# A decoder layer on one core: squares of the first norm off GpSimd and later, set-up of the samples' retention later, first key cache in steps, and the third up-projection pair's weight sums later

## The chip, the cores and the metric

One core of one Trainium2 chip runs the whole program. TensorE (PE) multiplies, VectorE (DVE) and GpSimd (POOL) do elementwise work, ScalarE (ACT) does activations and casts, and SyncE (SP) issues the transfers. Each engine works through its own queue in order and waits on semaphores for the others. The metric is the device time of one execution in microseconds; lower is better.

## The reference

One layer of a decoder for a prompt of 1024 tokens and 8 samples of 4 tokens, D = 1024, with the same weights (`D_FF` = 2816):

```python
h = _rmsnorm(x, norm_g)
p = h @ w_in
q, k, v, g, su, sv, xq, gt = jnp.split(p, cuts, axis=-1)
o_ret, S_new = _retention_branch(q, k, v, g, pos, S0, ret_gn_g, ret_chunk)   # 4 heads, rotary, decay, GroupNorm, silu(g)
o_sg, v_rows = _sgu_branch(jax.nn.gelu(su), jax.nn.gelu(sv), sg_ln_g, sg_ws, sg_bs)
o_x = _xattn(q=xq, mk, mv)          # 4 heads into 256 memory tokens; the samples have caches of their own
merged = sig(g_ret) * (o_ret @ w_br_ret) + sig(g_sg) * (o_sg @ w_br_sg) + sig(g_x) * (o_x @ w_br_x)
x = x + merged @ w_o
z = _rmsnorm(x, norm_ffn_g) @ w_up
a, b = split(causal_conv3(z))
x = x + (gelu(a) * b) @ w_down
y = _rmsnorm(x, norm_final_g)
```

Outputs are y for prompt and samples, the retention and convolution states, the memory keys and values, and the samples' gating rows. All of it is float32.

## The kernel before

**Data.** Prompt and samples lie side by side as T = 1056 columns, feature-major: eight tiles of 128 x 1056 in SBUF hold x (`xr[0..7]`). A float32 product is made of three matmuls on a high and a low part of each operand (`hh`, `hl` of the activations, `wh`, `wl` of the weights). Weights come in slabs of 512 KB (`w_dma`), ACT casts the high part and POOL subtracts for the low part (`w_prep`; a `wl<-wr,wh` row of POOL is one such split). A unit is one k-tile of one product: nine matmuls, three of them over each piece of the columns.

**Order.** Python code writes each engine's queue in advance; nothing is reordered later. Main products go unit by unit (`fm2` for q and k of head 0 interleaved, `fm` for others, `tm` token-major for V), and after each unit `hook()` advances the generators in `gens` by `rate` steps, one generator after the other, and runs what `later(n, ...)` put off by n units. `drain()` runs all steps that are left. Product tiles in PSUM (`mp`) have two buffers in the first half of the program, small ones (`ap`) two, the FFN's (`bp`) three.

**Entry.** For each x tile ACT writes `hh` and DVE writes `hl`. Then the tiles are squared in place and summed to `xr[7]`; `rstd_all` casts the sum to `rsh` (ACT), subtracts for `rsl` (DVE), sums over features by matmuls with ones, and makes `rst` = 1/rms with a Newton step (`rms`, `ry`). The norm is applied behind the products, so q, k and g of head 0 can run on raw x; V and later products need `rtok`, which is `rst` transposed. The generator `xnorm` does the part from `xr[4]` on, a step at a time, starting after `YA` units, and `YB` steps lie between squares and sum.

**Retention.** `retention(h, ...)` runs as a generator beside the next products: A (scores of a chunk pair, masked into `rt`), B (`rt` times V, the state's part), C (the gated result `ort`), and SA, SB, SC, SD for the samples. SA makes the samples' scores and the masked copies `s` and `kdm` that SC multiplies. The order of these steps is a tuple in the code.

**Gating unit and cross-attention.** `sgu` mixes channel groups: PE makes `ap<-sgW,vg`, DVE adds (`sgt`) and multiplies (`su`). `KS(h, i)` splits half of a head's cached keys (`kch` cast by ACT, `kcl` by POOL); `xattn` is a generator of 20-odd steps a head, in which `YA(i)` uses them.

**FFN.** The up-projection goes in pairs of 512 columns with seven products instead of eight: a11, a12, s4, s2, s3, s1, a22, where the s are sums of weight blocks (`f_sums`) and each part is split by `f_prep0` (a11, a12), `f_prep1` (s2, s3), `f_prep2` (s1, s4) and `f_prep3` (a22). `put` and `z_put` add a product in PSUM to tiles `zt`, `zu`, `z` on DVE. In pair 1, the second, DVE also still makes parts of the normed activations (`xl<-x2c,xh`); `Conv` steps follow the convolution of the pair before. The list `early1` says what of pair 1's weights is prepared in which unit of the last products ahead of the FFN.

Of the kernel before, what the change touches and what calls it, by code (L numbers as in the profile page):

```python
# [10 lines left out]
AF = mybir.ActivationFunctionType  # L11
ALU = mybir.AluOpType
# [66 lines left out]
def step_kernel(ctx: ExitStack, tc: tile.TileContext, xT, memT, wslab, cst, ident_d, rope, vec, sgc, sgm, sgs,  # L79
# [10 lines left out]
    def slot(name, dt=F32, shape=None):  # L90
        return sp.tile(shape or [P, T], dt, tag="S", name=name, bufs=NSLOT)
# [16 lines left out]
    def act(out, in_, func=AF.Identity, scale=1.0, bias=0.0, **kw):  # L108
        nc.scalar.activation(out=out, in_=in_, func=func, scale=scale, bias=bias, **kw)  # L109

    def vtt(out, a, b, op):
        nc.vector.tensor_tensor(out=out, in0=a, in1=b, op=op)  # L112

    def ptt(out, a, b, op):
        nc.gpsimd.tensor_tensor(out=out, in0=a, in1=b, op=op)  # L115
# [4 lines left out]
    def f(t):  # L120
        return t.bitcast(F32) if t.dtype == F32R else t
# [50 lines left out]
    gens = deque()  # L172
# [112 lines left out]
    def split(src, name, sub=ptt):  # L285
        shape = list(src.shape)
        hi = slot(name + "h", F32R, shape)
        lo = slot(name + "l", F32R, shape)
        nc.scalar.copy(out=hi, in_=src)
        sub(lo, src, f(hi), ALU.subtract)  # L290
        return hi, lo
# [60 lines left out]
    with tc.manual_schedule():  # L352
# [9 lines left out]
        xr = [slot("xr") for _ in range(8)]  # L362
# [43 lines left out]
            x_part(k, slice(0, T))  # L406

        for k in range(4):
            ptt(xr[k], xr[k], xr[k], ALU.mult)
            for a, b in {1: ((1, 0),), 3: ((3, 2), (3, 1))}.get(k, ()):  # L410
                ptt(xr[a], xr[a], xr[b], ALU.add)
        for i in range(2):
            hil[SLABS[i]] = first[i]
        wst.update(d=2, p=2, live=2)
# [8 lines left out]
        nc.vector.tensor_scalar(out=vecs[:, VBG:VBG + 32], in0=vecs[:, VBG:VBG + 32], scalar1=0.5, scalar2=None,  # L423
                                op0=ALU.mult)

        YA, YB = 5, 6

        def xnorm():
            for _ in range(YA):
# [64 lines left out]
        def retention(h, qt, kt, silu, V, st, s3, s0, s0s):  # L494
# [156 lines left out]
                    stt(ot[e][:, TP:T], a[:, e * 32:e * 32 + 32],  # L651
                        vecs[:, VGN + 2 * h + e:VGN + 2 * h + e + 1], silu[e][:, TP:T], ALU.mult, ALU.mult)

            for fn, *a in ((int,), (A, 0), (SA,), (A, 1), (B, 0), (B, 1), (SC, 0), (B, 2), (C, 0), (SC, 1), (A, 2), (B, 3),
                           (SB, 0), (B, 4), (C, 1), (A, 3), (B, 5), (SD,), (B, 6), (C, 2), (SB, 1), (B, 7),
                           (SB, 2), (SB, 3), (C, 3)):
                while defer:
                    defer.pop(0)()
                fn(*a)
                yield  # L660
# [217 lines left out]
        def sgu():  # L878
            for _ in range(3):
                yield  # L880
            for half in range(2):
                for g in range(4):
                    a = ap()
                    for n in range(4):
                        mm(a[:, n * P:(n + 1) * P], vt(4 * half + n)[:, g * P:(g + 1) * P], sgW[:, g * P:(g + 1) * P])
                    t = slot("sgt")
                    vtt(t[:, 0:512].rearrange("p (a b) -> p a b", a=4), a.rearrange("p (a b) -> p a b", a=4),
                        sgC[:, g * P:(g + 1) * P].unsqueeze(1).to_broadcast([P, 4, P]), ALU.add)
                    s = su[g][:, half * 512:(half + 1) * 512]
                    vtt(s, s, t[:, 0:512], ALU.mult)  # L890
                    yield
                if half == 0:
                    vc_load(0)
            a = ap()
            for g in range(4):
                mm(a[:, g * 32:g * 32 + 32], sgS[0:32, 512 + g * P:512 + (g + 1) * P],
                   sgS[0:32, 256 + 32 * g:256 + 32 * g + 32])
            t = slot("sgt")
            vtt(t[:, 0:128], a[:, 0:128], sgC[:, 512:640], ALU.add)
            for g in range(4):  # L900
                ptt(su[g][:, TP:T], su[g][:, TP:T], t[:, g * 32:g * 32 + 32], ALU.mult)
                later(4, lambda g=g: dma(scr[8 + g], su[g]))
            yield
# [25 lines left out]
        def KS(h, i):  # L929
            if h < H:  # L930
                ksl.setdefault(h, {})[i] = split(kcl[h][i], "kc")
# [184 lines left out]
        later(4, lambda: dma(sgv, sgS[0:32, 512:1024]))  # L1116
        rate[0] = 1.05
        gens.append(sgu())
        KS(0, 0)
        KS(0, 1)  # L1120
        gens.append(xattn(0))
        for m in range(1, 4):
            xq_unit(m)
# [76 lines left out]
        for m in range(8):  # L1200
# [4 lines left out]
            for half in range(2):  # L1205
                t = slot("mg", F32R)
                src = acc[m][:, half * HW:(half + 1) * HW]
# [73 lines left out]
        fraw, fw = {}, {}  # L1281
# [4 lines left out]
                for t, key in zip(fraw[j], (("up", j), ("up", NFF + j))):  # L1286
                    dma(t, wslab[SLABS.index(key)])

        def f_parts(j, names, src, own=False):
            if own:  # L1290
                hi, lo = slot("fh", F32R, [P, 1024]), slot("fl", F32R, [P, 1024])
            else:
                hi = wp.tile([P, 1024], F32R, tag="wh", name="wh", bufs=3)
                lo = wp.tile([P, 1024], F32R, tag="wl", name="wl", bufs=3)
            nc.scalar.copy(out=hi, in_=src)  # L1295
            ptt(lo, src, f(hi), ALU.subtract)
            for i, n in enumerate(names):
                fw[j][n] = (hi[:, 512 * i:512 * i + 512], lo[:, 512 * i:512 * i + 512])

# [5 lines left out]
        def f_sums(j, sub, sub34=ptt):  # L1305

            a11, a12, a21, a22 = f_quads(j)
            fsum[j] = (slot("fs"), slot("fs"))
            s2, s3, s1, s4 = [t[:, 512 * i:512 * i + 512] for t in fsum[j] for i in range(2)]
            sub(s1, a21, a22, ALU.add)  # L1310
            sub(s2, s1, a11, ALU.subtract)
            return lambda: (sub34(s3, a11, a21, ALU.subtract), sub34(s4, a12, s2, ALU.subtract))

        def f_prep0(j, own=False):
            fw[j] = {}
            f_parts(j, ("a11", "a12"), fraw[j][0], own)

        def f_prep1(j, own=False):
            f_parts(j, ("s2", "s3"), fsum[j][0][:, 0:1024], own)
# [4 lines left out]
        def f_prep3(j):  # L1324
            a22 = f_quads(j)[3]
            t = slot("f22", F32R)
            nc.scalar.copy(out=t[:, 0:512], in_=a22)
            ptt(t[:, 512:1024], a22, f(t)[:, 0:512], ALU.subtract)
            fw[j]["a22"] = (t[:, 0:512], t[:, 512:1024])
            del fraw[j]  # L1330
            if j > 1:
                f_dma(j + 1)


        def raw1():
            fraw[1] = [slot("fr", shape=[P, 1024]) for _ in range(2)]
            for t, key in zip(fraw[1], (("up", 1), ("up", NFF + 1))):
                dma(t, wslab[SLABS.index(key)])

        early1 = [int, lambda: f_prep0(1, True), lambda: f_sums(1, vtt, vtt)(), int, lambda: f_prep3(1),  # L1340
                  lambda: f_prep1(1, True), int, int]

        for half in range(2):
            rate[0] = 0.25
            for m in range(8):
                key = ("wo", m, half)
                hi, lo = w_get(key)
# [38 lines left out]
        def prod(w, name, ps=None, start=True, stop=True, tick=None):  # L1386


            if ps is None:
                ps = bpp.tile([P, 2, 512], F32, tag="bp", name="bp", bufs=3)  # L1390
            ch = ((0, 0, HA), (1, HA, HB)) if name in ("B12", "B22", "T1") else ((0, 0, QW), (1, QW, QW))
            wh, wl = [x.rearrange("p (k c) -> p k c", c=P) for x in w]
            for k in range(4):
                xh, xl = xop(name, k)
                for i, (a, r) in enumerate(((wh, xh), (wh, xl), (wl, xh))):
                    for q, c0, n in ch:
                        mm(ps[:, q, 0:n], a[:, k, :], r[:, c0:c0 + n], start=(start and k == 0 and i == 0),
                           stop=(stop and k == 3 and i == 2))
                if tick:
                    tick()  # L1400
            return ps

        def put(ps, out, tmp=None):
            if tmp is None:
                nc.scalar.copy(out=quarters(out), in_=ps[:, :, 0:QW])
            else:
                vtt(quarters(out), ps[:, :, 0:QW], quarters(tmp), ALU.add)
# [9 lines left out]
        def z_put(ps, half, z, zs, tmp=None):  # L1417

            if half == 0:
                put(ps, z[:, 2:2 + HW], tmp)  # L1420
                return
            oz = n496(z[:, 2 + HW:2 + TP])
            if tmp is None:
                nc.scalar.copy(out=oz, in_=ps[:, :, 0:HA])
                nc.scalar.copy(out=zs[:, :, 2:6], in_=by4(ps[:, 1, HA:HB]))
            else:
                vtt(oz, ps[:, :, 0:HA], n496(tmp), ALU.add)
                vtt(zs[:, :, 2:6], by4(ps[:, 1, HA:HB]), by4(tmp[:, 2 * HA:HW]), ALU.add)
# [51 lines left out]
        A = lambda k: (h_scale(k, 1), x_split(B1(k), k % 4, h(k, 1), None))  # L1480
# [84 lines left out]
        d = fw.pop(1)  # L1565
        p1, r, u3, u4 = blocks(1)
        put(prod(d["a11"], "B11", tick=do), p1)
        f_prep0(2)
        n = prod(d["a12"], "B21", tick=do)
        za = z_new(1)  # L1570
        z_put(n, 0, *za, p1)
        n = prod(d["s4"], "B22", tick=do)
        z_put(n, 1, *za)
        f_sums(2, ptt)()
        put(prod(d["s2"], "T2", tick=do), r, p1)
        f_prep1(2)
        pa.first()
        pa.tap(1)
        put(prod(d["s3"], "T3", tick=do), u3, r)
        pa.tap(0)  # L1580
        pa.gelu()
        f_prep2(2)
# [34 lines left out]
        for j in range(2, NFF):  # L1617
# [4 lines left out]
            d = fw[j]  # L1622
# [4 lines left out]
            p1, r, u3, u4 = blocks(j)  # L1627
# [355 lines left out]
```

## Time and profile before

| | |
|---|---|
| time, median of 3 runs | 1944.57 us (1942.96 to 1952.96) |
| profiled execution, its own time | 1949.1 us |
| span in the trace, mean granted clock | 1947.3 us, 0.987 |
| busy PE, DVE, POOL, ACT | 1878.4, 1078.1, 927.7, 615.9 us |
| HBM read, written | 137.04, 35.43 MB |

The span is from the first to the last instruction of the profiled execution; the 1.8 us between it and that execution's time lie outside. Rows of the timeline give start, duration in us, engine, line, operation, output<-inputs, shape, how many were joined (x6 means six in a row), and in brackets the engine's idle time before it and what ended that.

### The profile page before, as it was taken

Reading aid. Unit: us, or ns where it says so; the run is one execution under the profiler, and the core shown is the slowest. Engines: PE = TensorE matmul, PEld = TensorE weight load, DVE = VectorE, ACT = ScalarE, POOL = GpSimd, SP = SyncE. Lnnn points to the kernel's source line nnn. Section 1 sums busy time; section 2 is a strip of 40 time slices with the busy share of each in tenths; the row PEclk is TensorE's granted clock in tenths of the full one; section 3 lists DMA queues with packets and bytes.
Section 4 is the critical chain, followed back from the end, with each engine's and each line's share of the span. In section 5 each row is a group of like instructions: output and inputs, shape, how many; then the busy total and the mean of one; then the engine's idle time right before and its main releaser. Section 6 shows DMA issues by size and latency. Waiting matters only on the chain.

```text
span 1947.3 us, 31390 instructions
## 1 busy us (share of the span) xinstructions
PE 1878.4 (96%) x13201; PEld 1852.8 (95%) x13201; DVE 1078.1 (55%) x1506; ACT 615.9 (32%) x962; POOL 927.7 (48%) x576
## 2 busy tenths in 40 slices
PE   7999999999989999999999999899999999999997
PEld 6999999999989999999999999899999999999996
DVE  8463636443375541111112247999999999744446
ACT  5232232322234332111132233534434334321204
POOL 6242424232544334333154434477777777753404
PEclk9999999999999999999999999899999999999998
DMA  5112121324142313111221443022222222742202
GB/s 184 55 44 91 44 91 44 132 68 153 55 133 77 109 45 133 55 44 54 89 84 48 164 153 99 33 66 89 77 66 89 77 84 95 264 142 89 75 1 90
DMA packets 51741, 174.51 MB, mean 90 GB/s; under 512 B 5712, under 2 KB 8944, under 8 KB 51600
## 3 DMA queue, kind: packets, MB, share of 16 engines
q1 hardware_dynamic: 51600, 172.50, 26.3%
q8 instruction: 104, 1.70, 0.4%
q14 instruction: 37, 0.30, 0.1%
HBM read 137.04 MB, written 35.43 MB: 89 GB/s over the span
## 4 chain that ended last, share of the span: by engine, by line
PE 80%; DVE 11%; ACT 3%; issue 3%; DMA 1%; POOL 1%; SPq 0%; DVEq 0%; ACTq 0%; POOLq 0%
PE mp L106 55%; PE bp L106 20%; PE ap L106 4%; DVE xl L112 1%; DVE c L118 1%; DVE x2c L118 1%; DVE hl L118 1%; DVE s L112 1%; DMA xr<-in_xT 1%; DMA scr<-ox 0%; ACT sw L476 0%; DVE rt L118 0%; DVE st L526 0%; SPq L103 0%; PE ap L576 0%
## 5 line engine op out<-in xcount | busy, mean ns | idle before, releaser
L115 POOL TENSOR_TENSOR wl<-wr,wh 128x1024 fp32r<-128x1024 f32 x114 | 296.7, 2605 | 463.6 <-ACT wh L150 391.2
L106 PE MATMUL mp<-hh,wh 128*128 128x384 f32 (+1 forms) x1152 | 264.2, 337 | 9.7 <-DVE q L112 4.9
L106 PE MATMUL mp<-hl,wh 128*128 128x384 f32 (+1 forms) x1152 | 254.1, 328 | 4.8 <-DVE hl L118 4.8
L106 PE MATMUL mp<-hh,wl 128*128 128x384 f32 (+1 forms) x1152 | 251.8, 326 | 0.0
L106 PE MATMUL bp<-xh,wh 128*128 128x264 f32 (+2 forms) x1040 | 211.4, 284 | 1.0 <-DVE x2c L118 0.9
L106 PE MATMUL bp<-xl,wh 128*128 128x264 f32 (+2 forms) x1040 | 211.1, 284 | 0.0
L106 PE MATMUL bp<-xh,wl 128*128 128x264 f32 (+2 forms) x1040 | 211.0, 284 | 0.0
L106 PEld LDWEIGHTS mp<-hh,wh 128*128 128x128 f32 x1152 | 192.9, 192 | 12.9 <-ACT hh L109 5.3
L106 PEld LDWEIGHTS mp<-hl,wh 128*128 128x128 f32 x1152 | 193.5, 190 | 7.2 <-DVE hl L118 7.2
L106 PEld LDWEIGHTS mp<-hh,wl 128*128 128x128 f32 x1152 | 193.8, 190 | 0.0
L112 DVE TENSOR_TENSOR x<-x,mp 128x288 f32<-128x288 f32 (+3 forms) x167 | 105.7, 675 | 121.3 <-PE mp L106 121.3
L106 PEld LDWEIGHTS bp<-xh,wh 128*128 128x128 f32 x1040 | 162.4, 188 | 1.4 <-issue 1.4
L106 PEld LDWEIGHTS bp<-xl,wh 128*128 128x128 f32 x1040 | 162.4, 188 | 0.0
L106 PEld LDWEIGHTS bp<-xh,wl 128*128 128x128 f32 x1040 | 162.3, 188 | 0.0
L115 POOL TENSOR_TENSOR wl<-fs,wh 128x1024 fp32r<-128x1024 f32 x41 | 119.0, 2902 | 55.7 <-ACT wh L1295 55.7
L150 ACT CAST wh<-wr 128x1024 fp32r<-128x1024 f32 x100 | 103.9, 1041 | 78.7 <-PE mp L106 50.0
L106 PE MATMUL mp<-ach,whs 128*128 128x384 f32 (+3 forms) x524 | 124.3, 326 | 3.9 <-DVE x L112 3.1
L118 DVE SCALAR_TENSOR_TENSOR c<-z,hist,c 128x1024 f32<-128x1024 f32 x88 | 124.6, 1416 | 4.2 <-ACT c L109 2.5
L112 DVE TENSOR_TENSOR th<-mp,rst 128x768 f32<-128x768 f32 (+1 forms) x48 | 31.6, 701 | 170.9 <-PE mp L106 150.3
L106 PE MATMUL mp<-acl,whs 128*128 128x384 f32 (+3 forms) x524 | 124.1, 327 | 0.0
L106 PE MATMUL mp<-ach,wls 128*128 128x384 f32 (+3 forms) x524 | 124.0, 326 | 0.0
L118 DVE SCALAR_TENSOR_TENSOR th<-th,mp 128x768 f32<-128x768 f32 (+1 forms) x48 | 31.7, 701 | 145.4 <-PE mp L106 145.4
(356 smaller groups left out, 4107.9 us busy)
## 6 DMA issues: line engine op xcount, KB each, us to landing
wr<-in_wslab SPq DMA_DIRECT2D x162, 512.0 KB, 3.6
sca<-c SPq DMA_DIRECT2D x22, 528.0 KB, 3.0
opr<-sca SPq DMA_DIRECT2D x22, 528.0 KB, 4.5
opr<-scr SPq DMA_DIRECT2D x16, 528.0 KB, 5.4
scr<-ort SPq DMA_DIRECT2D x8, 528.0 KB, 7.6
x2c<-in_xT SPq DMA_DIRECT2D x8, 528.0 KB, 7.7
scx<-x2c SPq DMA_DIRECT2D x16, 264.0 KB, 3.5
x<-scx SPq DMA_DIRECT2D x8, 528.0 KB, 6.9
```

What stands on the lines that cost most here:

```text
L106: nc.tensor.matmul(out=out, lhsT=l, rhs=r, start=start, stop=stop)
L112: nc.vector.tensor_tensor(out=out, in0=a, in1=b, op=op)
L115: nc.gpsimd.tensor_tensor(out=out, in0=a, in1=b, op=op)
L118: nc.vector.scalar_tensor_tensor(out=out, in0=a, scalar=s, in1=b, op0=op0, op1=op1)
L150: nc.scalar.copy(out=hi, in_=raw)
```

## The change

Six edits.

```diff
         for k in range(4):
-            ptt(xr[k], xr[k], xr[k], ALU.mult)
+            act(xr[k], xr[k], AF.Square)
             for a, b in {1: ((1, 0),), 3: ((3, 2), (3, 1))}.get(k, ()):
-                ptt(xr[a], xr[a], xr[b], ALU.add)
+                vtt(xr[a], xr[a], xr[b], ALU.add)
...
-        YA, YB = 5, 6
+        YA, YB = 14, 3
...
-            for fn, *a in ((int,), (A, 0), (SA,), (A, 1), (B, 0), (B, 1), (SC, 0), (B, 2), (C, 0), (SC, 1), (A, 2), (B, 3),
+            for fn, *a in ((int,), (A, 0), (A, 1), (B, 0), (SA,), (B, 1), (SC, 0), (B, 2), (C, 0), (SC, 1), (A, 2), (B, 3),
...
         gens.append(sgu())
-        KS(0, 0)
-        KS(0, 1)
+
+        def first_keys():
+            for i in range(2):
+                KS(0, i)
+                yield
+                yield
+
+        gens.append(first_keys())
         gens.append(xattn(0))
...
-        early1 = [int, lambda: f_prep0(1, True), lambda: f_sums(1, vtt, vtt)(), int, lambda: f_prep3(1),
+        s34q = []
+        f_s12 = lambda: s34q.append(f_sums(1, vtt, vtt))
+        early1 = [int, lambda: (f_prep0(1, True), f_s12()), lambda: s34q[0](), int, lambda: f_prep3(1),
                   lambda: f_prep1(1, True), int, int]
...
         put(prod(d["a11"], "B11", tick=do), p1)
-        f_prep0(2)
         n = prod(d["a12"], "B21", tick=do)
         za = z_new(1)
         z_put(n, 0, *za, p1)
+        f_prep0(2)
         n = prod(d["s4"], "B22", tick=do)
         z_put(n, 1, *za)
+        put(prod(d["s2"], "T2", tick=do), r, p1)
         f_sums(2, ptt)()
-        put(prod(d["s2"], "T2", tick=do), r, p1)
-        f_prep1(2)
         pa.first()
         pa.tap(1)
         put(prod(d["s3"], "T3", tick=do), u3, r)
+        f_prep1(2)
```

`f_parts` and `f_prep0` also get a parameter `sub` for the subtracting engine, with the engine of before as default, which no call sets. Four squares go from POOL to ACT and three adds from POOL to DVE. The rest of the norm starts nine units later and has three steps fewer before its sum. SA stands behind B(0). The first two key splits become steps behind the gating unit's steps. Pair 1's first two sums stand a unit earlier than the other two. In pair 1, the preparation of pair 2 is issued later.

What stands in the queues there. First DVE at the entry, from just behind the six `hl` (`xr<-xr` are the adds of the sum of squares, `q` and `k` the evacuations of their products, `sw` the rotated half):

```order
+L112 TENSOR_TENSOR xr<-xr 128x1056 x3
 L423 TENSOR_SCALAR vecs<-vecs 128x32
-L112 TENSOR_TENSOR xr<-xr 128x1056 x4
 L112 TENSOR_TENSOR q<-mp,cosT 128x768
 L112 TENSOR_TENSOR q<-mp,cosT 128x288
-L112 TENSOR_TENSOR rsl<-xr,rsh 128x1056
+L112 TENSOR_TENSOR xr<-xr 128x1056
 L112 TENSOR_TENSOR k<-mp,cosT 128x768
 L112 TENSOR_TENSOR k<-mp,cosT 128x288
 L112 TENSOR_TENSOR q<-q,sw 128x1056
-L309 TENSOR_SCALAR rms<-ap 128x384
+L112 TENSOR_TENSOR xr<-xr 128x1056 x3
```

Three adds stand ahead of q's evacuation, one behind it and three behind k's; `rsl` follows them.

POOL at the end of the gating unit (`sgS` is the samples' part, `su` the samples' last multiplies), before:

```order
L115 TENSOR_TENSOR sgS<-sgS,sgW 32x512
L115 TENSOR_TENSOR kcl<-kc,kch 128x1024 x2
L115 TENSOR_TENSOR wl<-wr,wh 128x1024 x3
L115 TENSOR_TENSOR su<-su,sgt 128x32 x4
L115 TENSOR_TENSOR wl<-wr,wh 128x1024
L115 TENSOR_TENSOR vcl<-vc,vch 128x1024 x2
```

and now:

```order
L115 TENSOR_TENSOR sgS<-sgS,sgW 32x512
L115 TENSOR_TENSOR wl<-wr,wh 128x1024 x3
L115 TENSOR_TENSOR su<-su,sgt 128x32 x4
L115 TENSOR_TENSOR kcl<-kc,kch 128x1024 x2
L115 TENSOR_TENSOR wl<-wr,wh 128x1024
L115 TENSOR_TENSOR vcl<-vc,vch 128x1024 x2
```

The two key splits moved behind three weight splits and the samples' multiplies.

POOL in pair 1 (`z` and `zs` are the convolution's input tiles, `fs` the sums, `wl<-wr` here f_prep0's split, `wl<-fs` those of f_prep1 and f_prep2), before:

```order
L115 TENSOR_TENSOR wl<-wr,wh 128x1024
L1433 MEMSET z 128x2
L1434 COPY zs<-hist 128x8x2
L115 TENSOR_TENSOR fs<-wr 128x512
L115 TENSOR_TENSOR fs<-fs,wr 128x512
L115 TENSOR_TENSOR fs<-wr 128x512
L115 TENSOR_TENSOR fs<-wr,fs 128x512
L115 TENSOR_TENSOR wl<-fs,wh 128x1024 x2
```

and now:

```order
L1441 MEMSET z 128x2
L1442 COPY zs<-hist 128x8x2
L115 TENSOR_TENSOR wl<-wr,wh 128x1024
L115 TENSOR_TENSOR fs<-wr 128x512
L115 TENSOR_TENSOR fs<-fs,wr 128x512
L115 TENSOR_TENSOR fs<-wr 128x512
L115 TENSOR_TENSOR fs<-wr,fs 128x512
L115 TENSOR_TENSOR wl<-fs,wh 128x1024 x2
```

On POOL only f_prep0's split changed its place, by two small operations; the sums wait for other DVE operations than before, since the slots that they write come free in another order. On ACT the cast of f_prep1 (`wh<-fs`) stood ahead of the convolution's first activations (`c`):

```order
L1233 CAST xh<-x2c 128x528 x4
L1295 CAST wh<-fs 128x1024
L109 ACTIVATE c<-z,hist 128x1024
L109 ACTIVATE c<-zs,hist 128x32
L1455 COPY coll<-z 128x2
L1456 COPY coll<-zs 128x16
```

and stands behind them now:

```order
L1239 CAST xh<-x2c 128x528 x4
L109 ACTIVATE c<-z,hist 128x1024
L109 ACTIVATE c<-zs,hist 128x32
L1463 COPY coll<-z 128x2
L1464 COPY coll<-zs 128x16
L1301 CAST wh<-fs 128x1024
```

It moved behind four operations of ACT.

More of the change, by code (lines that the diff above doesn't have):

```diff
@@ L1287, in f_dma, with f_parts @@
                     dma(t, wslab[SLABS.index(key)])
-        def f_parts(j, names, src, own=False):
+        def f_parts(j, names, src, own=False, sub=ptt):
             if own:
@@ L1295, in f_parts @@
             nc.scalar.copy(out=hi, in_=src)
-            ptt(lo, src, f(hi), ALU.subtract)
+            sub(lo, src, f(hi), ALU.subtract)
             for i, n in enumerate(names):
@@ L1312, in f_sums, with f_prep0 @@
             return lambda: (sub34(s3, a11, a21, ALU.subtract), sub34(s4, a12, s2, ALU.subtract))
-        def f_prep0(j, own=False):
+        def f_prep0(j, own=False, sub=ptt):
             fw[j] = {}
-            f_parts(j, ("a11", "a12"), fraw[j][0], own)
+            f_parts(j, ("a11", "a12"), fraw[j][0], own, sub)
         def f_prep1(j, own=False):
```

## The prediction

> **What bounds the kernel.** I read the busy shares, then the chain of waits of TensorE, then each long wait in the timelines of the engines beside it.
>
> ```profile
> PE 1878.4 (96%) x13201; PEld 1852.8 (95%) x13201; DVE 1078.1 (55%) x1506; ACT 615.9 (32%) x962; POOL 927.7 (48%) x576
> PEclk9999999999999999999999999899999999999998
> ...
> PE ap L106 <- DVE sgt L112: 7.6, 1, 7.6
> PE bp L106 <- DVE zt L112: 6.9, 1, 6.9
> PE ap L106 <- DVE rt L118: 5.4, 3, 2.6
> PE mp L106 <- DVE q L112: 4.9, 1, 4.9
> ...
> PE mp L106 <- DVE hl L118: 4.8, 7, 1.7
> ...
> PE mp L106 <- DVE x2c L118: 2.8, 1, 2.8
> ```
>
> TensorE (PE) is busy 1878.4 of 1947.3 us, so 69 us of idle time is all that a reordering can reach, plus matmuls that run at a lower granted clock after an idle stretch. No matmul is added or removed. The second block is who ends PE's waits (total, times, longest): VectorE (DVE) nearly always. The change lies at the first five; they sum to 29.6 us. So the question at each is why DVE is late there, and what is late next.
>
> **Entry: squares off GpSimd (POOL), rest of the norm later.**
>
> ```profile
> 10.78 1.32 DVE L118 SCALAR_TENSOR_TENSOR hl<-xr,vecs,hh 128x1056 fp32r<-128x1056 f32 x1 [0.46 <-ACT hh L109]
> ...
> 13.23 18.96 DVE L118 SCALAR_TENSOR_TENSOR hl<-xr,vecs,hh 128x1056 fp32r<-128x1056 f32 x6
> ...
> 32.20 9.18 DVE L112 TENSOR_TENSOR xr<-xr 128x1056 f32<-128x1056 f32 x4
> ...
> 42.54 2.19 DVE L112 TENSOR_TENSOR rsl<-xr,rsh 128x1056 fp32r<-128x1056 f32 x1
> ...
> 12.18 18.90 POOL L115 TENSOR_TENSOR xr<-xr 128x1056 f32<-128x1056 f32 x6 [2.81 <-DVE hl L118]
> ...
> 36.74 0.65 PE L106 MATMUL mp<-hl,wh 128*128 128x384 f32 x3
> 37.23 0.65 PE L106 MATMUL mp<-hh,wl 128*128 128x384 f32 x3
> 42.76 1.22 PE L106 MATMUL mp<-hh,wh 128*128 128x384 f32 x3 [4.89 <-DVE q L112]
> ...
> 70.58 0.28 PE L106 MATMUL mp<-wh,hh 128*128 128x256 f32 x1
> ...
> 43.00:48.00 5.00, 5.00 (x18) 5.00 (x19) 4.99 (x4) 4.02 (x6) 3.83 (x3) 0.50 0.34 105
> ```
>
> One hl takes 1.32 us alone and 3.16 (18.96/6) while POOL's six squares and adds run; the two trade places, each held up by the other. Then four xr adds (9.18 us) stand ahead of q's evacuation, and PE, done with head 0's q and k at 37.88 (37.23 + 0.65), starts g only at 42.76. The granted clock in the next 5 us is 0.50: 2.5 us lost.
>
> After: POOL has no square here, so six hl at about 1.3 end near 13.2 + 7.9 = 21.1. The squares go to ScalarE (ACT), which already squares the other four tiles:
>
> ```profile
> 18.61 1.18 ACT L109 ACTIVATE hh<-xr,vecs 128x1056 fp32r<-128x1056 f32 x1
> 22.43 1.09 ACT L109 ACTIVATE xr<-xr 128x1056 f32<-128x1056 f32 x1 [2.64 <-DVE hl L118]
> ...
> 42.51 2.19 ACT L476 COPY sw<-mp 64x768 f32<-64x768 f32 x4
> 44.73 1.05 ACT L150 CAST wh<-wr 128x1024 fp32r<-128x1024 f32 x1
> ```
>
> Four more are 4.4 us behind ACT's last hh (18.61 + 1.18 = 19.8), so they end near 24.3, with the 2.64 of waiting gone; three adds behind them near 26, beside matmuls and well before q is to be evacuated. PE's hl waits (4.8) go: q and k end at 37.88 − 4.8 = 33.1, and g starts there, not at 42.76. From g's start to the first matmul of V PE took 70.58 − 42.76 = 27.8, 25.3 without the slow clock. With no new wait V would start at 58.4.
>
> New waits. The rstd matmuls stand in PE's queue behind the first unit of the second g half: nine units behind 33.1. Three matmuls start 0.49 after the three before them (36.74, 37.23), a unit is nine, so 1.46, and PE is there at 46.2. The sum they need is now made later: k's copies by ACT (2.2 behind 33.1), a weight cast and two squares (1.05 and 2 x 1.09) to 38.6, three adds, rsh (1.07), rsl. At 1.25 an add and 1.25 for rsl it is ready at 44.6. At 3.3 an add and 2.2 for rsl, with POOL's two wl and sw around, it is ready at 51.8. I take 48.5, near the middle: PE waits 2.3 (0 to 5.6). The clock falls behind such a wait:
>
> ```profile
> 205.69 1.62 PE L106 MATMUL ap<-V,rt 128*128 128x256 f32 x6 [2.64 <-DVE rt L118]
> ...
> 205.60:208.00 2.40, 2.31 (x9) 2.16 (x10) 1.22 (x4) 0.37 (x1) 0.55 (x2) 0.50 0.03 7
> ...
> 1182.85 0.72 PE L106 MATMUL mp<-mg,wh 128*128 128x264 f32 x4 [2.85 <-DVE x2c L118]
> ...
> 1182.00:1186.00 4.00, 3.15 (x26) 3.18 (x27) 3.29 (x5) 2.36 (x4) 1.59 (x1) 1.00 0.17 68
> ```
>
> A wait of 2.64 was followed by 0.50 for 2.4 us, one of 2.85 by none; I take 1.5. Last, the transposes for rtok now stand right before V, and V's first PSUM tile is the one g's first half gives back after rtok and two silu multiplies (2 x 0.65): 1.9 more. V starts at 58.4 + 2.3 + 1.5 + 1.9 = 64.1, **gain 6.5**; without the rsl wait 10.3, with 5.6 and 2.5 of clock 2.2.
>
> The Trainium skill, "TensorE: Matmul & The Clock Gate", section "What's actually happening", says that the clock halves after at least one idle window of about 3.4 us. The row at 205.69 differs (2.64, and 0.50 granted), the one at 1182.85 agrees; by the rule alone the 1.5 would go and the total be 18.
>
> **Samples' set-up (SA) later, four heads.**
>
> ```profile
> 106.75 2.46 DVE L112 TENSOR_TENSOR s<-s,cB 128x256 fp32r<-128x256 f32 x2
> ```
>
> SA's four DVE operations (1.54, 0.19, 2.46; the first and third beside POOL) stood ahead of the rt of A(1) that B(1) needs. Behind B(0) they delay SC(0) instead, one unit after B(1). The three rt waits (5.4) and some clock go. What comes instead: SA's first step on ACT starts one unit later, SC(0) stands two further on, so by my walk through each head's timeline 1.9, 0.8 and 2.0 of its chain stick out. I take **0**, between the full 5.4 + 1.5 with nothing new and −3, where all of the late chain sticks out.
>
> **First key cache in steps.**
>
> ```profile
> 538.03 10.57 DVE L112 TENSOR_TENSOR su<-su,sgt 128x512 f32<-128x512 f32 x1
> ...
> 549.23 0.69 DVE L112 TENSOR_TENSOR su<-su,sgt 128x512 f32<-128x512 f32 x1
> ...
> 538.79 4.66 POOL L115 TENSOR_TENSOR kcl<-kc,kch 128x1024 fp32r<-128x1024 f32 x2
> 543.42 4.62 POOL L115 TENSOR_TENSOR wl<-wr,wh 128x1024 fp32r<-128x1024 f32 x2
> ...
> 549.25 1.01 PE L106 MATMUL ap<-sgW,vg 128*128 128x128 f32 x3 [7.58 <-DVE sgt L112]
> ...
> 549.00:555.00 6.00, 5.75 (x29) 5.75 (x30) 3.87 (x7) 1.05 (x1) 0.70 (x1) 0.63 0.87 247
> ```
>
> One su multiply, 0.69 alone, takes 10.57: it is held until POOL's four splits, back to back, are over (543.42 + 4.62 = 548.04). PE resumes 1.2 us later and loses 2.2 to the clock. The change moves both kcl behind the gating unit's last step; two wl remain. If DVE is again held to the end of POOL's run, that is 538.8 + 4.6 = 543.4, PE resumes at 544.6: 4.6 gained and about 0.5 of clock, **5.1**. If it gets in behind the first, 2.3 more and all of the clock: 9.6. If the two casts, now issued without kch ahead, let the third wl in too, 2.4 less: 2.7.
>
> The kcl find POOL behind the four small su, near 562 to 567; the first matmul on them is four to five units behind the last step, where POOL has only wl. Cross-attention's steps come four units (5.8 us) later, and fit: 92 steps on 92.4 that the hooks of the remaining gate units give. Its last results are needed only after the first gc and all bs products. I take 0 (±2).
>
> The Trainium skill, "SBUF — State Buffer", section "Who interferes with whom", says that a VectorE instruction with two SBUF inputs and a GpSimd one that reads SBUF exclude each other for a whole instruction. The 10.57 agrees, but it outlasts four instructions, which the rule does not say; if one instruction were all, the total would be 21.
>
> **Pair 1's sums in two units.** PE's 2.85 at 1182.85 stays: DVE is full there, and the two early sums only change the order ahead of it. Two 0.7 us sums: **0** (±1.5).
>
> **Third pair's sums later.**
>
> ```profile
> 1235.27 14.57 DVE L112 TENSOR_TENSOR xl<-x2c,xh 128x528 fp32r<-128x528 f32 x10
> 1249.77 0.69 DVE L112 TENSOR_TENSOR zt<-bp,zt 128x528 f32<-128x528 f32 x1
> ...
> 1238.88 1.69 POOL L115 TENSOR_TENSOR fs<-wr 128x512 f32<-128x512 f32 x1 [1.26 <-DVE xl L112]
> ...
> 1246.79 2.48 POOL L115 TENSOR_TENSOR wl<-fs,wh 128x1024 fp32r<-128x1024 f32 x1 [1.10 <-ACT wh L1295]
> ...
> 1250.61 0.78 PE L106 MATMUL bp<-xh,f 128*128 128x264 f32 x2 [6.93 <-DVE zt L112]
> ...
> 1251.00:1257.00 6.00, 6.00 (x31) 6.00 (x31) 4.83 (x11) 3.65 (x5) 1.08 (x1) 0.54 0.01 3
> ```
>
> Ten xl, 0.70 alone elsewhere,
>
> ```profile
> 1172.15 0.70 DVE L112 TENSOR_TENSOR xl<-x2c,xh 128x528 fp32r<-128x528 f32 x1
> ```
>
> take 14.57, 7.6 too many, beside POOL's four sums (1238.88 to 1245.69) and its wl (1246.79 to 1249.27). The put of s2's product stands behind them and lets PE go at 1250.61, 6.93 late, and then at 0.54 of the clock for 6 us (2.8). After: the sums wait for a slot freed four DVE operations later, and the cast ahead of wl stands behind the convolution's first step, so wl (2.1 of the excess) and part of the sums leave. Some excess stays: f_prep0's wl is issued later and now meets the first xl. Put at about 1246.1 − 0.7: gain 4.4, and 0.5 of the clock, **4.9**. Bounds: 1, if wl and sums only change places, and 6.9 + 2.8 = 9.7. What is late next: nothing that I see; s3, s1 and a22 of the second pair stand between this place and the third pair's first product.
>
> **Sum.** 6.5 + 0 + 5.1 + 0 + 4.9 = 16.5. The profiled execution took 1949.1 us, so 1932.6 in such an execution; it lies 4.5 over the median of the runs, 1944.57, and against this I say **1928.1**.
>
> **Rivals.**
> Small gain: the entry's gain turns into the rsl wait (2.2), and su is held through a third wl (2.7), with 2 at the third pair: 6.8, time 1938. For it: each of my gains is at a place where the two engines share, and moving work has it meet the next operation.
> Large gain: DVE gets in between POOL's instructions, as hl did with POOL's squares at 13 to 32: 10.3 + 9.6 + 6 = 26 less 2 for SA, time 1921. Against it: su waited through four in a row.
> Slower: the norm's chain decides. All of V waits for rtok, which needs rsl, then the rstd matmuls, three Newton operations and the transposes. If POOL holds DVE there as it held su (10.57 for one operation) in two of the five operations after k's evacuation, rsl is ready near 48.5 + 20, PE waits 22 and loses 2.5 of clock: V starts at 58.4 + 22 + 2.5 + 1.9 = 84.8, 14.2 later than before, and with the 10.0 from the other places the time is 1949. It is slower than before once rsl is ready after about 64. Against it: POOL has only three instructions in that stretch (wl, sw, wl), not back to back.
> No effect: the third pair's wait is set by ACT's casts, not by POOL, and su by its PSUM tile; then only the entry is left, 1938, inside the first rival. The 10.57 speaks against it.
>
> **Chances.** My forecast (gain 11 to 21) 0.49, small gain 0.23, large 0.21, slower 0.07. 0.5% is 9.7 us, about what a measurement can tell from no change: faster than 1934.8 in the forecast and the large gain, and a little of the small, 0.71; same 0.24; slower than 1954.3, the slower rival's far end and what I missed, 0.05. The range reaches from the large gain's end, 1917, to the small gain's, 1941; the forecast's own is 1923 to 1934.
>
> **What would show it.** The six hl at 1.3 each and g's first matmul near 33; a new PE wait near 46, ended by rsl; V's first matmul at 62 to 66. PE's waits for rt gone, others for s or the state's PSUM of at most 2 each. su at about 6 instead of 10.57 and PE's wait there near 3. xl's ten in about 11 and the wait for zt at 2 to 3. Wrong, if one su still takes 8 or more, if V starts after 70, or if a wait over 4 us stands where there was none, in the cross-attention above all.

## The result, and the profile after

| | before | after |
|---|---|---|
| median (lowest to highest), 6 runs each | 1945.11 us (1942.77 to 1952.96) | 1931.77 us (1928.54 to 1934.71) |
| ratio, 95% interval | 1 | 0.9919 (0.9906 to 0.9932) |
| profiled execution, its own time | 1949.1 us | 1929.98 us |
| span, mean granted clock | 1947.3 us, 0.987 | 1928.2 us, 0.994 |

The ratio is 15.8 us of 1945.11 (13.2 to 18.3); the two medians of the table differ by 13.3 (0.9931), at the small end of that interval. Forecast were a gain of 16.5 and a time of 1928.1: the measured median lies 3.7 above that, inside the forecast's own 1923 to 1934. The two traces are 19.1 apart, since the execution profiled before lay 4.0 above its median and the one after 1.8 below.

The page after, busy shares and granted clock:

```profile
PE 1870.1 (97%) x13201; PEld 1844.8 (96%) x13201; DVE 1055.6 (55%) x1509; ACT 620.0 (32%) x966; POOL 913.3 (47%) x569
...
PEclk9999999999999999999999999999999999999998
```

PE is 8.3 us less busy with the same 13201 matmuls: the mean granted clock rose from 0.987 to 0.994, which is about 52 us at half clock before and 22 after. Its idle time fell by 10.8. PE's waits now, the ones that answer to those shown of before and the new ones (total, times, longest):

```profile
PE ap L106 <- DVE s L112: 4.3, 3, 1.6
...
PE ap L106 <- DVE xql L112: 3.8, 2, 2.1
...
PE ap L106 <- DVE sgt L112: 3.0, 1, 3.0
PE mp L106 <- DVE x2c L118: 2.6, 2, 2.0
PE bp L106 <- DVE z L112: 2.1, 1, 2.1
...
PE mp L106 <- DVE silu L112: 1.5, 1, 1.5
...
PE ap L106 <- ACT rsh L333: 1.4, 1, 1.4
...
PE bp L106 <- DVE zs L112: 1.1, 1, 1.1
...
PE ap L106 <- DVE rsl L112: 0.9, 1, 0.9
```

The five waits of before, 29.6 us (7.6, 6.9, 5.4, 4.9, 4.8), are 3.0 now: only sgt is left. In their place stand s, xql (0.5 before), z, silu, rsh, zs and rsl, 15.1 together. (A sixth long wait of before, 4.8 for the first hh, ends at the program's first matmul; no edit touches it, and it varies with the execution.) The main matmuls, those that write `mp` or `bp`, come in the same order in both programs. The start of the same matmul in the two traces, counted from 0, tells how far after is ahead:

| main matmul | before | after | ahead | the stage's part |
|---|---|---|---|---|
| first of the program | 4.84 | 5.77 | -0.9 | |
| first of g, head 0 | 42.76 | 32.36 | 10.4 | |
| first of V, head 0 | 70.58 | 63.62 | 7.0 | entry 7.0 |
| behind the retention (no. 1800) | 356.06 | 344.79 | 11.3 | retention 4.3 |
| behind the wait at su (no. 3015) | 550.99 | 534.86 | 16.1 | su 4.9 |
| behind the cross-attention (no. 3760) | 731.79 | 717.77 | 14.0 | -2.1 |
| ahead of the third pair (no. 7140) | 1241.96 | 1227.97 | 14.0 | 0.0 |
| first of a22 of pair 1 (no. 7152) | 1250.61 | 1229.97 | 20.6 | |
| a22 of pair 2 (no. 7320) | 1275.09 | 1257.84 | 17.3 | pair 1 to 2: 3.3 |
| last | 1932.68 | 1914.32 | 18.4 | 1.1 |

The timelines after, at the three places. The entry, DVE, then PE in front of the rstd matmuls and of V:

```profile
13.47 7.92 DVE L118 SCALAR_TENSOR_TENSOR hl<-xr,vecs,hh 128x1056 fp32r<-128x1056 f32 x6
...
39.81 6.04 DVE L112 TENSOR_TENSOR xr<-xr 128x1056 f32<-128x1056 f32 x3
...
47.02 0.44 PE L106 MATMUL ap<-rsh,ones 128*128 128x384 f32 x1 [1.41 <-ACT rsh L333]
48.31 0.45 PE L106 MATMUL ap<-rsl,ones 128*128 128x384 f32 x1 [0.85 <-DVE rsl L112]
...
63.62 0.39 PE L106 MATMUL mp<-wh,hh 128*128 128x256 f32 x1 [1.54 <-DVE silu L112]
```

Six hl take 7.92 instead of 18.96. The rstd matmuls wait 1.41 + 0.85 = 2.3, V's first 1.5.

The end of the gating unit, DVE, POOL, PE:

```profile
526.84 5.99 DVE L112 TENSOR_TENSOR su<-su,sgt 128x512 f32<-128x512 f32 x1
...
527.59 4.69 POOL L115 TENSOR_TENSOR wl<-wr,wh 128x1024 fp32r<-128x1024 f32 x2
...
533.49 0.86 PE L106 MATMUL ap<-sgW,vg 128*128 128x128 f32 x4 [2.95 <-DVE sgt L112]
```

su ends 0.55 behind the second split (532.83 and 532.28): held again to the end of POOL's run, which is shorter by two instructions.

Pairs 1 and 2, DVE, POOL, PE:

```profile
1221.34 7.87 DVE L112 TENSOR_TENSOR xl<-x2c,xh 128x528 fp32r<-128x528 f32 x10
...
1237.39 1.53 DVE L112 TENSOR_TENSOR z<-z,zu 128x496 f32<-128x496 f32 x1
1238.85 2.40 DVE L112 TENSOR_TENSOR zs<-zs,zu 128x32 f32<-128x32 f32 x1
...
1236.01 5.18 POOL L115 TENSOR_TENSOR wl<-fs,wh 128x1024 fp32r<-128x1024 f32 x2
...
1229.97 0.49 PE L106 MATMUL bp<-xh,f 128*128 128x264 f32 x2 [0.38 <-ACT c L109]
...
1237.62 0.48 PE L106 MATMUL bp<-xh,wh 128*128 128x264 f32 x2 [1.12 <-DVE zs L112]
1243.29 0.51 PE L106 MATMUL bp<-xh,wh 128*128 128x264 f32 x2 [2.13 <-DVE z L112]
```

The ten xl take 7.87 instead of 14.57 and PE's wait of 6.93 is 0.38. Then POOL's two splits stand beside DVE's additions to z and zs; the last one, on 32 columns, takes 2.40, and PE waits 1.12 and 2.13.

### The profile page after: what moved, and what is told of

Same layout as the page of the kernel before. It is cut to its first block, busy times and chain, and to the rows that moved or that the text cites. A ratio compares the mean times of both kernels' runs of the same rounds, so it can differ in the third digit from the quotient of the medians.

```text
span 1928.2 us, 31394 instructions
## 1 busy us (share of the span) xinstructions
PE 1870.1 (97%) x13201; PEld 1844.8 (96%) x13201; DVE 1055.6 (55%) x1509; ACT 620.0 (32%) x966; POOL 913.3 (47%) x569
## 4 chain that ended last, share of the span: by engine, by line
PE 80%; DVE 11%; ACT 4%; issue 3%; POOL 1%; DMA 0%; DVEq 0%; SPq 0%; ACTq 0%; POOLq 0%
PE mp L106 56%; PE bp L106 20%; PE ap L106 4%; DVE c L118 1%; DVE xl L112 1%; DVE x2c L118 1%; ACT sw L476 1%; ACT wh L150 0%; DVE ssf L112 0%; DVE fs L112 0%; DVE st L526 0%; DVE rt L118 0%; PE ap L576 0%; DVE x L112 0%; DVE th L112 0%
```

## Experiments: each part alone

All ratios are to the kernel before, with runs on the same chip. Four kernels have one part of the change each.

**The entry alone** (both of its edits).

```diff
-            ptt(xr[k], xr[k], xr[k], ALU.mult)
+            act(xr[k], xr[k], AF.Square)
...
-                ptt(xr[a], xr[a], xr[b], ALU.add)
+                vtt(xr[a], xr[a], xr[b], ALU.add)
...
-        YA, YB = 5, 6
+        YA, YB = 14, 3
```

> The kernel before with only the entry's two edits: the four squares and three adds off GpSimd, and YA, YB = 14, 3. Theory (DVE's hl and xr adds are held by GpSimd's two-input operations): V's first matmul near 63.6, as in the changed kernel, 7 us earlier than before; waits for rt in the retention stay at 5.4, so the whole gain is about 7 us, ratio 0.9964. Rival (the gain of 3.9 us that the changed kernel makes in the retention comes from the entry's shift against the weight splits, not from SA's place): waits for rt are shorter here too, gain about 11, ratio 0.9943.

Ratio 0.9955 (0.9942 to 0.9969). V's first matmul at 62.81, 7.8 earlier, and 7.3 at the last matmul. The waits for rt stay:

```profile
PE ap L106 <- DVE rt L118: 5.4, 3, 2.7
```

So what the changed kernel gains in the retention is not the entry's.

**SA alone.**

```diff
-            for fn, *a in ((int,), (A, 0), (SA,), (A, 1), (B, 0), (B, 1), (SC, 0), (B, 2), (C, 0), (SC, 1), (A, 2), (B, 3),
+            for fn, *a in ((int,), (A, 0), (A, 1), (B, 0), (SA,), (B, 1), (SC, 0), (B, 2), (C, 0), (SC, 1), (A, 2), (B, 3),
```

> The kernel before with only SA moved behind B(0). Theory (SA's place alone makes the retention's 3.9 us: the waits for rt of 5.4 go with their slow clock, waits for s of 4.3 come with less): gain 3 to 4 us, ratio 0.998. Rival (the prediction's: nothing, since the late s costs what the early rt gains): ratio 1.000.

Ratio 0.9982 (0.9973 to 0.9991). The retention gains 3.2 us, and 2.7 are left at the last matmul. rt is gone from the waits, and s came:

```profile
PE ap L106 <- DVE s L112: 4.3, 3, 1.6
```

The theory holds and the prediction's 0 falls: a gain of 1.1 in waits, the rest slow clock. It had followed the 2.64 for rt (and, at 157.5, a wait for ort, which SA's place does not touch), and did not follow the first wait for s, 1.57 at 106.70 in the changed kernel, whose stretch behind it has the granted clock at 1.00:

```profile
106.70 0.30 PE L106 MATMUL ap<-s0h,s 128*64 128x256 f32 x1 [1.57 <-DVE s L112]
...
106.00:111.00 5.00, 4.30 (x30) 4.30 (x31) 2.96 (x8) 3.61 (x6) 2.16 (x3) 1.00 0.00 0
```

**The first keys alone.**

```diff
-        KS(0, 0)
-        KS(0, 1)
...
+        gens.append(first_keys())
         gens.append(xattn(0))
```

> The kernel before with only the first key cache as steps behind the gating unit. Theory: su is held until GpSimd's two remaining wl are over, near 6 us instead of 10.57; PE's wait for sgt 3.0 instead of 7.6, gain 8 us up to about 575 us; then the cross-attention, four steps later, gives back 5 by waits for xql and pt; in all 3 us, ratio 0.9983. Rival (the 5 us given back in the cross-attention come from the entry's shift and not from the four steps): gain 7 to 8, ratio 0.996.

Ratio 0.9990 (0.9981 to 0.9999). Up to the matmul behind su it gains 7.8, of which 2.4 had come in the retention, where nothing is edited (slow clock behind the waits for ort, there in one trace and not in the other); so 5.4 at su. A stage's part in one pair of traces is uncertain by that much: the retention of the changed kernel gains 4.3 in its own trace, and of the seven further runs below with the same retention code six gain 2.7 to 2.8 and one 4.4. The same waits as in the changed kernel appear in the cross-attention, without the entry's shift:

```profile
PE ap L106 <- DVE xql L112: 3.7, 2, 2.1
...
PE ap L106 <- DVE sgt L112: 3.0, 1, 3.0
...
PE ap L106 <- DVE pt L112: 1.5, 3, 0.9
```

What is given back belongs to this edit: 8.9 ahead behind su (no. 3030), 6.7 behind the cross-attention, so 2.2 and not the theory's 5. Another 2.4 go near 1176, to slow clock behind the wait for x2c, which this edit does not touch.

**The third pair's preparation alone.**

```diff
-        f_prep0(2)
         n = prod(d["a12"], "B21", tick=do)
         za = z_new(1)
         z_put(n, 0, *za, p1)
+        f_prep0(2)
...
-        f_sums(2, ptt)()
         put(prod(d["s2"], "T2", tick=do), r, p1)
-        f_prep1(2)
+        f_sums(2, ptt)()
...
         put(prod(d["s3"], "T3", tick=do), u3, r)
+        f_prep1(2)
```

> The kernel before with only the third pair's preparation issued later. Theory (GpSimd's sums meet the convolution's taps and the z additions instead of the xl): the wait for zt of 6.9 shrinks to under 1, two new waits for zs and z of 3 us in all come 8 to 13 us later; gain 3 us, ratio 0.998. Rival (the new waits come from another phase, brought by the earlier parts of the change): no new waits, gain 8, ratio 0.996.

Ratio 0.9975 (0.9964 to 0.9985). At the a22 product 6.7 us are gained (no. 7140 to 7152), and the two new waits come, 1.15 and 2.16, at the same places as in the changed kernel:

```profile
1252.39 0.48 PE L106 MATMUL bp<-xh,wh 128*128 128x264 f32 x2 [1.15 <-DVE zs L112]
...
1258.05 0.51 PE L106 MATMUL bp<-xh,wh 128*128 128x264 f32 x2 [2.16 <-DVE z L112]
```

From no. 7140 to a22 of pair 2, 3.3 are left (-0.8 to 2.5 us ahead). The theory holds. The four ratios multiplied give 0.9902, with an interval of some 0.002 to either side by their own intervals, and the whole change has 0.9919 (0.9906 to 0.9932): the parts add up, within the intervals.

**The squares without the later norm.** The first two pairs of lines of the entry's edit; `YA, YB` stay 5, 6.

> The kernel before with only the four squares and three adds off GpSimd; YA, YB stay 5, 6. Theory (the entry's gain needs both halves): the six hl take 7.9 instead of 18.96 and PE's hl waits of 4.8 go, but the second four squares and their adds still stand ahead of q's evacuation on DVE, so g's first matmul waits for q, 2 to 4 us with a slow clock after it; gain 4 to 6 us, ratio 0.9975. Rival (the squares alone do it, the later norm only trades the q wait for the rsl wait): gain 7, ratio 0.9964.

Ratio 0.9979 (0.9970 to 0.9988). DVE, then PE:

```profile
13.68 7.93 DVE L118 SCALAR_TENSOR_TENSOR hl<-xr,vecs,hh 128x1056 fp32r<-128x1056 f32 x6
...
26.75 9.36 DVE L112 TENSOR_TENSOR xr<-xr 128x1056 f32<-128x1056 f32 x4
...
37.50 0.98 PE L106 MATMUL mp<-hh,wh 128*128 128x384 f32 x2 [4.72 <-DVE q L112]
```

The theory holds: the squares alone free hl and bring g 5.3 us forward, and the wait for q stays. It is 4.72, more than the 2 to 4 expected, since the four xr adds ahead of q's evacuation take 9.36. V starts 5.3 earlier, against 7.8 with both: the later norm is worth 2.4, by 5.8 gained at g and 3.3 given back at rsl and silu.

**Pair 1's sums in one unit again** (the changed kernel without that edit).

```diff
-        early1 = [int, lambda: (f_prep0(1, True), f_s12()), lambda: s34q[0](), int, lambda: f_prep3(1),
+        early1 = [int, lambda: f_prep0(1, True), lambda: f_sums(1, vtt, vtt)(), int, lambda: f_prep3(1),
```

> The changed kernel with pair 1's four sums all in one unit again. Theory (these two sums' place costs nothing either way): the wait for x2c near 1169 is 2.0 to 2.9, no difference over 1 us. Rival (the 1 us that the changed kernel gains between 1168 and 1190 over the parts measured alone is this edit's): 1 us slower there.

Ratio 0.9927 (0.9915 to 0.9940), not separable from the changed kernel. In the trace the difference at that place is 2.4 us: the wait is one of 2.85 as before, not 0.66 and 1.96, and this time the clock fell behind it:

```profile
1168.00:1171.00 3.00, 1.01 (x9) 0.80 (x7) 3.00 (x5) 1.12 (x2) 0.00 (x0) 1.00 0.44 162
1171.00:1177.00 6.00, 5.14 (x23) 5.17 (x24) 5.29 (x6) 2.36 (x4) 2.63 (x1) 0.52 0.11 45
```

The second row has the granted clock at 0.52 for 6 us; in the kernel before the same wait of 2.85 was followed by 1.00. So the difference is more than the theory's 1 us, by the clock. The other traces show how often: the wait of 2.8 to 3.0 stands here in all seven kernels with the sums in one unit, and half clock follows in five of them, which lose 1.2 to 2.4 us here against the trace of the kernel before. Of the seven kernels with two units, two lose 1.2. So the 0.0 of the table is the luck of one trace; over these fourteen the edit is worth about 1 us here.

## Experiments: the causes, on the changed kernel

No ratio here can be told from the changed kernel's 0.9919 (0.9906 to 0.9932); what these runs show stands in their traces.

**What holds su.** The two splits beside it go to DVE.

```diff
-LO_DVE = [k for i, k in enumerate(SLABS) if k[0] in ("km", "vm") and i % 2] + [("sv", 0, 0), ("sv", 0, 1)]
+LO_DVE = [k for i, k in enumerate(SLABS) if k[0] in ("km", "vm") and i % 2] + [("sv", 0, 0), ("sv", 0, 1), ("xq", 2), ("xq", 3)]
```

> The changed kernel with the two weight splits that run on GpSimd beside the first su (slabs xq 2 and 3) on DVE instead, ahead of sgt and su in its queue. Theory (su is held until GpSimd's run of two-input operations is over): su takes 0.7 instead of 5.99; DVE spends 2 x 1.25 on the splits; PE's wait for sgt falls from 3.0 to under 1, about 3 to 4 us faster up to the cross-attention. Rival (su waits for something else, its PSUM tile or the sgt before it, at that place): su stays near 5 and PE's wait grows by the 2.5 us of splits.

Ratio 0.9907 (0.9893 to 0.9921). DVE, POOL, PE:

```profile
527.44 2.34 DVE L112 TENSOR_TENSOR wl<-wr,wh 128x1024 fp32r<-128x1024 f32 x2
...
530.42 1.04 DVE L112 TENSOR_TENSOR su<-su,sgt 128x512 f32<-128x512 f32 x1
...
527.66 3.25 POOL L115 TENSOR_TENSOR sgS<-sgS,sgW 32x512 f32<-32x512 f32 x1 [0.71 <-DVE sgS L874]
```

su: 10.57 beside four splits, 5.99 beside two, 1.04 beside none. The cause is shown. Now DVE's run holds POOL: sgS takes 3.25 instead of 1.27, and su ends 0.55 behind it (531.46 and 530.91), as it ended 0.55 behind the splits. PE's wait for sgt is 0.95. From no. 2900, ahead of su, to no. 3030 behind it the trace gains 8.5 on the kernel before; the changed kernel gains 4.9. Of these 3.6 the whole time shows nothing that can be told from the changed kernel's.

**The phase of the cross-attention**, that is in which units its steps fall. One `yield` behind each key split, not two.

```diff
                 KS(0, i)
                 yield
-                yield
```

> The changed kernel with one step instead of two behind each of the first key splits, so that the cross-attention starts two units later than in the kernel before and not four. Theory (the 5 us lost in the cross-attention are a matter of phase: with four steps the xql subtraction of the next head lands behind the gates' evacuations on DVE): the waits for xql of 3.8 and pt of 1.5 shrink by about half, a wait for kcl of up to 1 us appears at the first YA; 0 to 3 us faster than the changed kernel. Rival (the loss comes from PE running 10 us ahead of the other engines, whatever the phase): the same waits, no difference.

Ratio 0.9925 (0.9912 to 0.9939). The wait for xql falls to 0.5, but others come:

```profile
PE ap L106 <- DVE pt L112: 2.3, 2, 2.0
...
PE ap L106 <- DVE y L112: 2.1, 1, 2.1
...
PE ap L106 <- DVE ox L1001: 0.7, 1, 0.7
```

So phase sets which operation is late, as the theory has it, and the sum stays the same, as the rival has it: PE's waits from no. 3030 to no. 3760 are 5.7 us, 5.4 in the changed kernel and 3.8 in the kernel before. No wait for kcl came. Neither is fully right, and why the later start costs these waits stays open.

**The second squares four units earlier**.

```diff
-        YA, YB = 14, 3
+        YA, YB = 10, 7
```

> The changed kernel with YA, YB = 10, 7: the second four squares start four units earlier, the place of the rstd matmuls in PE's queue stays. Theory (the wait of 2.3 in front of the rstd matmuls comes from the late squares): rsl is ready 3 to 5 us earlier, the wait and its 1.5 us of slow clock go, V's first matmul at 60 instead of 63.6; about 3 us faster. Rival (the added adds now stand ahead of q's evacuation and beside GpSimd's splits, and hold g's first matmul): a new wait for q at 32 of 1 to 3 us, no gain.

Ratio 0.9924 (0.9912 to 0.9937), no gain. DVE:

```profile
33.10 8.41 DVE L112 TENSOR_TENSOR xr<-xr 128x1056 f32<-128x1056 f32 x3 [0.74 <-ACT xr L109]
...
46.00 3.40 DVE L112 TENSOR_TENSOR rsl<-xr,rsh 128x1056 fp32r<-128x1056 f32 x1
```

Three adds, 6.04 in the changed kernel, take 8.41, and rsl 3.40 instead of 1.26; rsl is ready at 49.4, later than before the edit (48.25), and the wait in front of the rstd matmuls is 3.07 instead of 2.3. POOL runs sw, wl, sw, wl without a pause from 31.09 to 43.80 there. Both theories miss: no wait for q came, and what moved earlier took longer beside POOL.

**The third pair's sums on DVE**.

```diff
-        f_sums(2, ptt)()
+        f_sums(2, vtt, vtt)()
```

> The changed kernel with the third pair's four sums on DVE (0.7 each, 2.8 in all) instead of GpSimd. Theory (the two new waits for zs and z, 3.3 us, are DVE's small operations held by GpSimd's sums and splits): with the sums gone from GpSimd its two splits come earlier and the zs addition falls from 2.4 towards 0.2; the waits for zs and z shrink, 1 to 3 us faster. Rival (DVE has no room there: it is busy without a pause from 1214 to 1252, and 2.8 us more is 2.8 us later): the waits grow by up to 2.8, slower than the changed kernel by 1 to 3.

Ratio 0.9929 (0.9917 to 0.9942). The additions take 0.66 and 0.18 and the waits for zs and z nearly go, but PE waits for zu ahead of them:

```profile
1239.41 0.71 PE L106 MATMUL bp<-xh,wh 128*128 128x264 f32 x2 [3.33 <-DVE zu L112]
```

The additions were held by POOL, as the theory says. DVE has no room for the sums, as the rival says: ahead of zu they take 2.6 (1232.69 to 1235.30), and a tap (one step of the convolution) of 32 columns that starts beside POOL's split takes 2.32 instead of 1.27. From no. 7140 to a22 of pair 2 the trace gains 2.0, the changed kernel 3.3.

**The sums and both splits one product later** (with the two splits of the gating unit on DVE).

```diff
         put(prod(d["s2"], "T2", tick=do), r, p1)
-        f_sums(2, ptt)()
...
-        f_prep1(2)
         pa.tap(0)
         pa.gelu()
-        f_prep2(2)
...
         vtt(za[1][:, :, 2:6], za[1][:, :, 2:6], by4(u4[:, 2 * HA:HW]), ALU.add)
+        f_sums(2, ptt)()
         pb.first()
         pb.tap(1)
+        f_prep2(2)
+        f_prep1(2)
```

> The changed kernel with the two splits on DVE as in the run before with them, and the third pair's sums and their two splits one product later still, behind the additions to z and zs. Theory (the waits for zs and z are DVE's additions held by GpSimd): both go, 3.3 us and about 1.5 of clock; the sums meet the second convolution's taps, where nothing waits at once; in all 3 to 5 us faster than the changed kernel, ratio 0.989. Rival (GpSimd's chain is then too late for the third pair's third product, which needs s4): a new wait of 2 to 6 us for wl or fs near 1250, no gain or a loss.

Ratio 0.9936 (0.9922 to 0.9950). The waits for zs and z go, as the theory says. But the rival sets the time, at another place than it says: s2 of the third pair is its second product, and waits at once.

```profile
1241.34 0.81 PE L106 MATMUL bp<-xh,wh 128*128 128x264 f32 x2 [5.88 <-ACT wh L1301]
...
1245.70 0.59 PE L106 MATMUL bp<-xh,wl 128*128 128x264 f32 x1 [3.10 <-POOL wl L115]
```

In the changed kernel that product waits 0.10 for the same split, so in this order of products the sums have no room to come later.

**Only the split of s1 and s4 later** (again with the gating unit's two on DVE).

```diff
         pa.gelu()
-        f_prep2(2)
         n = prod(d["s1"], "T1", tick=do)
...
         pb.tap(0)
+        f_prep2(2)
         conv_end(0, pa, pb)
```

> The changed kernel with the two splits on DVE, and in pair 1 only f_prep2(2), the split of s1 and s4, issued after the last tap instead of ahead of the s1 product. Theory (GpSimd's second wl<-fs, 1238.4 to 1241.2, holds DVE's additions to z and zs, and with them the wait of 2.13; its result is needed only four products on): the wait for z goes with its slow clock, about 3 us faster there and 1 to 2 at su, ratio 0.990 or less. Rival (DVE is held by whatever GpSimd does, and the split meets the taps instead): the wait moves by some us and stays near 2, only the 1 to 2 us at su remain.

Ratio 0.9909 (0.9895 to 0.9922), median 1929.9. The wait for z falls from 2.13 to 0.66, the last zs addition from 2.40 to 0.18; then waits of 0.96 (zt on ACT), 1.42 (zt) and 2.04 (zu) come in front of s3, s1 and a22 of pair 2, and by then the gain is used up (2.4 from no. 7140, 3.3 in the changed kernel). The rival describes it: the wait moves. Of the versions run, this one and the one with two splits on DVE have the lowest ratios, inside the changed kernel's interval.

## Why the prediction was right, point by point

The forecast holds in its size, and its mechanism holds at the entry, at su and for the wait it named at the third pair. Three steps failed: SA, the cross-attention, and what is late next at the third pair.

- **hl and the squares.** Six hl at 7.92 (said 7.9), g's first matmul at 32.36 (33.1), shown by the run with the squares alone to be POOL's doing.
- **The new waits at the entry.** 2.3 in front of the rstd matmuls (2.3), 1.5 in front of V (1.9), V at 63.62 (64.1); the gain of 7.0 (6.5) comes with a first matmul 0.9 later. That rsl is ready at 48 was the middle of two bounds, 44.6 and 51.8, so the match is in part luck. The run with earlier squares shows that the late squares alone do not set it: with them earlier, the adds and rsl take 4.5 longer beside POOL.
- **SA.** 0 was said; with SA alone the retention gains 3.2, and the ratio is below 1 through its interval. The step that failed: that the late s costs what the early rt gains. The waits were sized right (4.7 said, 4.3), and the prediction's own terms, 5.4 + 1.5 - 4.7, give 2.2; the 0 left out that the clock fell behind the wait of 2.64 for rt and not behind those for s (1.6 at most).
- **The first keys.** At su 4.9 (5.1): held to the end of POOL's run, the first of three cases. The bound of 9.6 for the second case counts 0.5 of clock twice: 4.6 + 2.3 + 2.2 is 9.1. The cross-attention was taken at 0 (±2); it gave back 2.1 here and 2.2 with the keys alone. The step that failed: it asked whether the later steps still fit, not what DVE does where they now fall. Waits for xql and pt came (5.2 together, 0.8 before), more than the waits for y and ox that went (2.8).
- **The third pair.** 3.3 (4.9). The wait that was named went wholly: 6.6 at a22, more than the 4.4. Some excess of the xl was to stay (ten in about 11, a wait of 2 to 3); they take 7.87, since the first sum starts only at 1227.43, near their end at 1229.21. The step that failed is "What is late next: nothing that I see": z and zs additions were next, and the claim that three products stand ahead of the third pair's first was wrong, since s3 and s1 had left PE and s2 of the third pair is its second product.
- **Pair 1's two sums.** 0 (±1.5); 0.0 between the two traces, and about 1 us over all fourteen, by the clock behind the wait for x2c. The time does not resolve it.

In the traces the errors are +4.3 (retention, where some 1.5 is the luck of a trace without slow clock behind ort), -2.1 (cross-attention), -1.6 (third pair), +1.1 (behind it) and +0.3 (entry and su), in all 18.4 against 16.5: the sum is better than its terms, because they cancel.

## What to carry to other kernels

Where two engines hold each other up, read from the timeline which of the loser's operations PE waits for, and move the other engine's work away from that one operation; then look at what it meets at the new place, because four of the five parts here gave back something there. For a two-input operation of VectorE that starts beside a run of GpSimd instructions, take the whole run as the upper bound of its cost: su was held through all of it, hl only through one instruction at a time. Once the long waits are gone, shifting the work by some units only changes which operation is late.

## What the hardware showed that was not expected

- A DVE operation of 0.69 was held for as many POOL instructions as stood in a row: 10.57, 5.99 and 1.04 us beside four, two and no splits. At the entry the two engines traded places instruction by instruction (hl 3.16 each beside squares). What decides between the two is open.
- The granted clock behind a wait is not a matter of its length alone: 2.85 at the same place was followed by 1.00 in the kernel before and by 0.52 over 6 us in the run with pair 1's sums in one unit; 2.64 by 0.50, 1.57 by 1.00. The Trainium skill, "TensorE: Matmul & The Clock Gate", section "What's actually happening", gives a window of about 3.4 us that runs free of the program; the two outcomes of one wait agree with a free-running window, while drops behind 2.64 and 2.85 are under its length. The clock records of these traces show what decides. In each of the fourteen, all slow stretches begin on one grid with a step of 3.413 us. Take PE's idle time in each step of that grid, up to 1900 us and where the clock is full: of the 71 steps that slow clock follows, 70 have 1.93 us or more and one 1.86; of the 7603 others none has more than 1.88. (At the program's end, behind 1900 us, eight of 19 have less than 1.93, down to 1.36.) The wait of 2.85 in the kernel before fell across two steps, so each has PE busy for about 2.0 of 3.41 (idle 1.40 and 1.45); with the sums in one unit again, one step has it busy for 1.20, and the next step is slow (two rows of the kernel before, then two of that run):

```profile
1178.00:1181.41 3.41, 2.01 (x17) 1.79 (x15) 3.41 (x7) 0.63 (x1) 0.00 (x0) 1.00 0.51 154
1181.41:1184.83 3.41, 1.97 (x16) 2.00 (x17) 2.70 (x6) 2.22 (x3) 0.42 (x1) 1.00 0.20 79
...
1167.81:1171.22 3.41, 1.20 (x10) 0.99 (x9) 3.41 (x7) 1.26 (x2) 0.00 (x0) 0.99 0.40 145
1171.22:1174.63 3.41, 2.77 (x12) 2.80 (x13) 2.70 (x4) 2.21 (x3) 1.23 (x1) 0.50 0.20 79
```

So behind a wait near 2 us, such as the two of 1.99 for ort, the clock is slow in one execution and not in another: after both in the kernel before (from 157.5 and 345.2), after neither with the first keys alone. A step at half clock costs up to 1.7 us, as much as the smaller parts of this change.
